# RMS norms scaled by rows and transposed plainly, a weight split in placed pieces, more fillers, and output projections that end in token order

## The chip, the cores and the metric

The kernel is one program on 1 core of a Trainium2 chip. The metric is the device time of one execution in microseconds (us). The engines that matter are TensorE (PE, matmuls, with its weight loads listed as PEld), VectorE (DVE), ScalarE (ACT), GpSimd (POOL) and the DMA queues, which SyncE (SP) issues nearly all. Each engine works through its own queue; engines wait for each other by semaphores.

## The reference, cut to what matters

256 tokens of width 1024 pass two blocks. The first block has two layers, and each layer a mixer (stick-breaking attention in layer 0, retention in layer 1) and a mixture of 16 experts. The second block has an S5 branch and a sparse attention branch, merged, and then a large expert lookup (PEER). Norms stand between all of them.

```python
def first_block(x, c, ...):
    for i in range(2):
        shift, scale, gate = adaln_params(c, ada_w[i, 0], ada_b[i, 0])
        h = x * (1.0 + scale) + shift
        y = stick_breaking_attention(h, w_in, w_out) if i == 0 else retention(h, ...)   # both end in  o @ w_out
        x = layer_norm(ALPHA * x + (1.0 + gate) * y, ln_g[i, 0], ln_b[i, 0])
        shift, scale, gate = adaln_params(c, ada_w[i, 1], ada_b[i, 1])
        y = grouped_moe(x * (1.0 + scale) + shift, ...)      # top 2 of 16 experts in one of 4 groups
        x = layer_norm(ALPHA * x + (1.0 + gate) * y, ln_g[i, 1], ln_b[i, 1])

def rmsnorm(x, g):
    return x * rsqrt(mean(x * x) + 1e-6) * g

def second_block(x, ...):
    proj = rmsnorm(x, norm1_g) @ w_in                        # first rms norm
    ...                                                      # S5 and attention branches, merged
    h = x + merged @ w_out
    h = h + peer_ffn(rmsnorm(h, norm2_g), ...)               # second rms norm, then PEER
    return rmsnorm(h, norm_f_g)
```

## The kernel before, in words

**Tiling.** The 256 tokens are two token tiles, t = 0 and 1, of 128 rows. Between stages the activations lie with tokens on partitions (`x_mid`); for a projection they are transposed in 8 blocks of 128 columns to a tile with the width on partitions. The dense projections split each f32 operand into a high half (an ACT cast to fp32r) and a low half (the difference, by DVE or POOL) and add three matmuls (`split` L148, `mm3` L166). Weights come in pieces of 1 MB; each takes a buffer `w` and two buffers `hl`, of which block 1 has 6 and 6 and the mixers' part of block 2 has 3 and 4.

**Order.** The kernel is traced in program order, and a planner orders each engine's queue by program priority and its own estimate of when work is ready. `issue_after(ins)` (also through `behind()`, L340, for the last DVE instruction traced) keeps what it encloses behind an instruction on that instruction's engine. A tile pool of four PSUM banks, `ps`, serves all short uses, another of four, `y`, the accumulators.

**Output projections** (`proj_out` L427) take the weight two blocks of rows at a time: 4 chunks for stick-breaking attention and for the merge, 8 for retention. In a chunk token tile 0's 12 matmuls come first, then token tile 1's 12, into four accumulators `y[t][half]`. So in the last chunk tile 0 is complete 12 matmuls before tile 1.

**Layer norms** (`layer_norm` L304) follow for each token tile: product with the gate row on DVE (L314), sum with the residual (L316), mean and sum of squares on ACT (L320, L324), the power -1/2 on POOL (L330), the scaling on DVE (L335, or L332 and L333 in the last one, which also applies the gain and bias). `warm` (L172) puts fillers on PE: products with a matrix of ones into a bank that nobody reads; `WA` says how many at each place. A filler is two matmul instructions of 128 columns. After the norms ahead of the experts come 16 transposes, the router's logits, the routing on DVE, and the gather. `moe` keeps 15 MB of expert weights in flight and loads the next piece where a buffer comes free; its first loads take the buffers that `proj_out` gives back.

**RMS norms** (`normed` L993) sum the squares of each token tile on ACT (L1000), take the power on POOL (L1005), and make a diagonal matrix of the row scales (L1007). A matmul of a block of `x` with this diagonal transposes and scales it at once, block by block, both token tiles into one PSUM bank; ACT then writes the high half with the gain (L1012) and DVE the low half (L1013). The first rms norm is called from `mixers` (L1312), which prefetches the first weight `wa[0]` ahead of it, its low half in four DVE pieces (L160), and `wa[1]` behind it. The second is called from `block2` ahead of `peer_scores` (L1414), whose first weight has its low half made by POOL in four pieces (L160).

## Time and profile before

| what | value |
|---|---|
| median of 3 runs | 2079.44 us (2075.39 to 2080.48) |
| profiled execution, own time | 2080.8 us |
| its span, first to last instruction | 2079.0 us |
| mean granted clock of PE | 0.977 |
| PE busy, share of the span | 1970.1 us, 95% |
| PE weight loads | 1531.0 us, 74% |
| DVE | 1218.3 us, 59% |
| ACT | 801.3 us, 39% |
| POOL | 417.7 us, 20% |
| DMA | 496.09 MB, mean 239 GB/s |

The busy times overlap. PE's includes the modelled end of each pipelined matmul, so 95% does not say that PE is at its peak. The chain of waits is the work followed back from the last instruction, at each step to what released it. A granted clock of 1.00 is PE at 2.4 GHz, 0.50 is 1.2 GHz. In a timeline a row merges neighbouring instructions of one kind: its start, its length, the engine, the line, what it writes and reads, and how many.

### The profile page before, as it was taken

How to read it: one execution, taken by the hardware profiler on the slowest of the kernel's cores; microseconds unless marked ns; L12 is line 12 of the kernel's file. 1: busy time of each engine (PE TensorE's matmuls, PEld its weight loads, DVE VectorE, ACT ScalarE, POOL GpSimd, SP SyncE). 2: the span in 40 equal slices, each digit the busy share in tenths (PEclk: the TensorE clock that was granted, in tenths of full speed). 3: DMA queues.
4: the chain of work that ended last, by engine and by line, in shares of the span. 5: the costliest groups of instructions: out<-in, count | busy, mean ns of one | idle time of the engine just before them, and what ended most of it. 6: DMA issues, size and time to landing. Idle time of an engine off the chain costs nothing.

```text
span 2079.0 us, 31873 instructions
## 1 busy us (share of the span) xinstructions
PE 1970.1 (95%) x12566; PEld 1531.0 (74%) x12567; DVE 1218.3 (59%) x2489; ACT 801.3 (39%) x1254; POOL 417.7 (20%) x319
## 2 busy tenths in 40 slices
PE   6999999989999999997888999999999999999998
PEld 4977443339998844335766889999999998888886
DVE  3645321128885422115587569767999986555555
ACT  3444111124454211113333544555444444444444
POOL 1000000002332000000231144544665550000000
PEclk8999999999999899998998999999999999999999
DMA  9797799997875699996332361544554445555554
GB/s 388 270 407 269 293 395 392 395 384 252 312 266 178 241 370 394 396 391 257 132 132 72 131 238 35 161 151 143 171 193 145 153 153 191 186 190 192 189 189 149
DMA packets 155888, 496.09 MB, mean 239 GB/s; under 512 B 10177, under 2 KB 10593, under 8 KB 147153
## 3 DMA queue, kind: packets, MB, share of 16 engines
q1 hardware_dynamic: 152880, 483.42, 64.6%
q0 software_dynamic: 2848, 10.53, 1.4%
q8 instruction: 102, 1.67, 0.3%
q14 instruction: 58, 0.47, 0.1%
HBM read 486.30 MB, written 7.61 MB: 238 GB/s over the span
## 4 chain that ended last, share of the span: by engine, by line
PE 76%; DVE 8%; ACT 2%; issue 2%; DMA 1%; POOL 1%; POOLq 0%; SPq 0%; DVEq 0%; ACTq 0%
PE ps L163 45%; PE y L163 28%; PE y L1200 1%; PE ps L187 1%; DMA w<-moe_w_down 1%; DVE pair L1547 1%; DVE hl L153 1%; DVE et L1471 1%; DVE i L1448 0%; ACT hl L151 0%; POOL hl L160 0%; DVE ps L1193 0%; DVE pos L1459 0%; DVE v L1447 0%; DVE t L725 0%
## 5 line engine op out<-in xcount | busy, mean ns | idle before, releaser
L163 PE MATMUL ps<-hn,pair 128*128 128x256 f32 x3072 | 383.3, 285 | 4.2 <-DVE pair L1547 4.1
L163 PEld LDWEIGHTS ps<-hn,pair 128*128 128x128 f32 x3072 | 373.8, 192 | 5.4 <-DVE pair L1547 4.9
L163 PE MATMUL ps<-w,t 128*64 128x512 f32 x624 | 278.9, 598 | 7.7 <-ACT t L196 2.7
L163 PE MATMUL ps<-hl,t 128*64 128x512 f32 x624 | 279.7, 599 | 4.5 <-DVE t L194 3.1
L1547 POOL TENSOR_TENSOR pair<-raw,pair 128x640 fp32r<-128x640 f32 x128 | 235.9, 1851 | 157.0 <-ACT pair L1545 150.8
L151 ACT CAST hl<-w 128x2048 fp32r<-128x2048 f32 x79 | 150.4, 1903 | 137.0 <-PE ps L163 81.3
L153 DVE TENSOR_TENSOR pair<-raw,pair 128x1024 fp32r<-128x1024 f32 x128 | 156.8, 1225 | 67.2 <-ACT pair L151 67.2
L163 PE MATMUL y<-pair,tmp 128*128 128x512 f32 x768 | 189.7, 395 | 0.0
L163 PE MATMUL y<-pair,eT 128*128 128x512 f32 x768 | 186.5, 391 | 0.0
L163 PEld LDWEIGHTS y<-pair,tmp 128*128 128x128 f32 x768 | 144.4, 188 | 33.9
L163 PEld LDWEIGHTS ps<-w,t 128*64 128x64 f32 x624 | 82.4, 137 | 117.2 <-issue 106.8
L163 PEld LDWEIGHTS y<-pair,eT 128*128 128x128 f32 x768 | 144.2, 188 | 32.4
L1545 ACT CAST pair<-raw 128x1024 fp32r<-128x1024 f32 x128 | 134.2, 1051 | 65.1 <-PE ps L163 24.6
L153 DVE TENSOR_TENSOR hl<-w,hl 128x2048 fp32r<-128x2048 f32 x51 | 118.2, 2318 | 52.8 <-ACT hl L151 49.2
L151 ACT CAST pair<-raw 128x1024 fp32r<-128x1024 f32 x128 | 133.8, 1045 | 1.1 <-issue 1.1
L163 PEld LDWEIGHTS ps<-hl,t 128*64 128x64 f32 x624 | 81.6, 137 | 68.8 <-issue 62.1
L163 PE MATMUL ps<-hl,a 128*128 128x256 f32 x1008 | 130.3, 287 | 1.8 <-ACT hl L151 1.8
L330 POOL TENSOR_TENSOR ln_st<-ln_st,c_mhalf 128x1 f32<-128x1 f32 x8 | 7.9, 982 | 604.0 <-ACT ln_st L327 604.0
L163 PEld LDWEIGHTS ps<-hl,a 128*128 128x128 f32 x1008 | 124.0, 191 | 6.1 <-ACT hl L151 2.0
L725 DVE TENSOR_TENSOR t<-t,ps 128x512 f32<-128x512 f32 x16 | 11.0, 688 | 171.5 <-PE ps L163 171.5
L163 PEld LDWEIGHTS ps<-a,hl 128*128 128x128 f32 x864 | 106.4, 195 | 3.5 <-issue 1.6
L163 PE MATMUL ps<-a,hl 128*128 128x256 f32 x864 | 108.6, 287 | 0.3 <-DVE a L153 0.3
(427 smaller groups left out, 3012.5 us busy)
## 6 DMA issues: line engine op xcount, KB each, us to landing
raw<-peer_u SPq DMA_DIRECT2D x128, 512.0 KB, 3.5
raw<-peer_v SPq DMA_DIRECT2D x128, 512.0 KB, 3.3
w<-ada_w SPq DMA_DIRECT2D x35, 1024.0 KB, 8.3
w<-moe_w_down SPq DMA_DIRECT2D x28, 1024.0 KB, 14.3
hl<-moe_w_down SPq DMA_DIRECT2D x28, 1024.0 KB, 14.2
w<-moe_w_up SPq DMA_DIRECT2D x26, 1024.0 KB, 14.3
hl<-moe_w_up SPq DMA_DIRECT2D x26, 1024.0 KB, 14.3
w<-moe_w_gate SPq DMA_DIRECT2D x24, 1024.0 KB, 14.4
```

Source lines behind the costliest of these rows:

```text
L151: nc.scalar.copy(hi, src)
L153: nc.vector.tensor_tensor(lo, src, hi.bitcast(F32), op=OP.subtract)
L163: self.last_mm = self.nc.tensor.matmul(out, lhsT=lhsT, rhs=rhs, start=start, stop=stop, skip_group_check=True)
L187: self.nc.tensor.transpose(out, in_, self.ident[:in_.shape[0], :in_.shape[0]])
L330: nc.gpsimd.tensor_tensor(st[:, 3:4], st[:, 2:3], self.mhalf[:, 0:1], op=OP.pow)
L725: nc.vector.tensor_tensor(hid, hid, pu, op=OP.mult)
L1200: self.nc.tensor.matmul(py[32 * q:32 * q + 32, :S], lhsT=self.s5_ct[ct][:, 4 * i + q], rhs=ab[q % 2][:, x, ri], start=j == 0, stop=j == 3, ...
L1471: V.tensor_reduce(et[:, 0:2, h], oh.rearrange("p a k j -> p a j k"), axis=AX.X, op=OP.add)
L1545: nc.scalar.copy(up[:, 0], ur)
L1547: lo = eng.tensor_tensor(up[:, 1, ks], ur[:, ks], up[:, 0, ks].bitcast(F32), op=OP.subtract)
```

## The change

`proj_out` keeps the last two chunks of the weight and runs their matmuls together: all 24 of token tile 0, then all 24 of token tile 1, which are queued behind tile 0's. It applies to the two output projections of the first block and to the merge projection. `normed` scales the rows of a token tile on DVE (one instruction of 128x1024 in place of the diagonal), transposes its 8 blocks with PE's transpose into four PSUM banks taken at the start, tile 0 and then tile 1, and then evacuates block by block; DVE's steps and ACT's are held in program order. The first rms norm's weight `wa[0]` has its low half in four DVE pieces at set places: before the norm, after the rows of tile 0, after block 3 and after block 5; `wa[1]` is queued behind the norm on ACT too. Fillers: 5 for 3 after tile 0's sum of squares in every layer norm, 7 and 5 after the two tiles of the last layer norm, 4 after tile 0's squares in each rms norm.

```diff
--- before.py
+++ after.py
@@ -40,8 +40,10 @@
 TH = 1
 LNP = ((0, 1), (1, 1))
 WN = 128
-WA = {4: 3, 5: 3, 6: 3, 7: 3, (2, 0): 1, (3, 0): 3}
+WA = {4: 3, 5: 3, 6: 3, 7: 3, (2, 0): 1, (3, 0): 5}
 LAG = 2
+RW = (4, 0)
+LW = (7, 5)
 ATR = 4
 SCORE = 4.16
 PACE = 2.81
@@ -331,11 +333,19 @@
             if last:
                 V.scalar_tensor_tensor(x[:, t], xh[:, t], st[:, 1:2], grow, op0=OP.add, op1=OP.mult)
                 self.tail = V.scalar_tensor_tensor(x[:, t], x[:, t], st[:, 3:4], brow, op0=OP.mult, op1=OP.add)
+                self.warm(x[:, t], LW[t])
             else:
                 V.tensor_scalar(xh[:, t], xh[:, t], st[:, 1:2], st[:, 3:4], op0=OP.add, op1=OP.mult)
         if not last:
             self.left = [(t, s, x, grow, brow) for t in range(T) for s in (slice(0, 512), slice(512, D))]
         return xh
+
+    def after(self, *ops):
+
+        stack = ExitStack()
+        for op in ops:
+            stack.enter_context(self.tc.issue_after(op.ins))
+        return stack
 
     def behind(self):
 
@@ -401,6 +411,17 @@
         for src in chunks:
             self.done[src.tensor.name, src.offset] = self.wload(src, eng=eng)
 
+    def slices(self, src):
+
+        w, hi, lo = (a.rearrange("p (k n) -> p k n", k=KB) for a in (self.w(), self.hl(), self.hl()))
+        self.nc.sync.dma_start(w, src)
+        self.nc.scalar.copy(hi, w)
+        self.done[src.tensor.name, src.offset] = hi, lo
+
+        def piece(q):
+            self.nc.vector.tensor_tensor(lo[:, q], w[:, q], hi.bitcast(F32)[:, q], op=OP.subtract)
+        return [lambda q=slice(k, k + 2): piece(q) for k in range(0, KB, 2)]
+
     def proj_t(self, src, x, emit, pool=None, eng=None):
 
         wh, wl = self.wload(src, eng=eng)
@@ -428,19 +449,25 @@
 
         nkb = o[0].shape[1]
         W = src.rearrange("(k p) n -> p k n", p=P)
+        held = {}
         for k2 in range(nkb // 2):
             between.get(k2, lambda: None)()
             w, wh, wl = (a.rearrange("p (k n) -> p k n", k=2) for a in (self.w(), self.hl(), self.hl()))
             self.nc.sync.dma_start(w, W[:, k2 * 2:k2 * 2 + 2])
             self.split(wh, wl, w)
-            for t in range(T):
-                for kk in range(2):
-                    k = k2 * 2 + kk
-                    oh, ol = o[0][:, k, t * P:t * P + P], o[1][:, k, t * P:t * P + P]
-                    for hf in range(2):
-                        cs = slice(hf * 512, hf * 512 + 512)
-                        self.mm3(y[t][hf], (oh, ol), (wh[:, kk, cs], wl[:, kk, cs]),
-                                 first and k == 0, last and k == nkb - 1)
+            for kk in range(2):
+                held[k2 * 2 + kk] = wh[:, kk], wl[:, kk]
+
+            if not (last and k2 == nkb // 2 - 2):
+                for t in range(T):
+                    with self.tc.issue_after(self.last_mm.ins) if t and len(held) > 2 else nullcontext():
+                        for k, (h, l) in held.items():
+                            oh, ol = o[0][:, k, t * P:t * P + P], o[1][:, k, t * P:t * P + P]
+                            for hf in range(2):
+                                cs = slice(hf * 512, hf * 512 + 512)
+                                self.mm3(y[t][hf], (oh, ol), (h[:, cs], l[:, cs]),
+                                         first and k == 0, last and k == nkb - 1)
+                held = {}
             self.background(self.rate)
 
 
@@ -990,28 +1017,39 @@
                                     op0=OP.subtract, op1=OP.mult)
 
 
-    def normed(self, x, gcol, hl=None):
+    def normed(self, x, gcol, hl=None, among=()):
 
         self.pieces = PC[1]
         nc, V = self.nc, self.nc.vector
-        xs, scales = self.act8().rearrange("p (t d) -> p t d", t=T), []
+        xs, among = self.act8().rearrange("p (t d) -> p t d", t=T), dict(among)
+
+        def place(name):
+            if name in among:
+                with self.behind():
+                    among[name]()
+        place("first")
+        pts = [self.psum((P, 2, S)) for _ in range(KB // 2)]
         for t in range(T):
-            rs = self.wk.tile([P, 2], F32, name="rms")
-            nc.scalar.activation(xs[:, t], x[:, t], AF.Square, accum_out=rs[:, 0:1])
-            if SM & 4:
-                nc.scalar.activation(rs[:, 0:1], rs[:, 0:1], AF.Identity, scale=1.0 / D, bias=self.eps[:, 1:2])
-            else:
+            rs, junk = self.wk.tile([P, 2], F32, name="rms"), self.t4()
+            nc.scalar.activation(junk, x[:, t], AF.Square, accum_out=rs[:, 0:1])
+            self.warm(junk, RW[t])
+            with self.behind():
                 V.tensor_scalar(rs[:, 0:1], rs[:, 0:1], 1.0 / D, RMS_EPS, op0=OP.mult, op1=OP.add)
             nc.gpsimd.tensor_tensor(rs[:, 1:2], rs[:, 0:1], self.mhalf[:, 0:1], op=OP.pow)
-            scales.append(self.wk.tile([P, P], F32, name="rms_diag"))
-            V.tensor_scalar(scales[t], self.ident, rs[:, 1:2], None, op0=OP.mult)
+            with self.behind():
+                V.tensor_scalar(xs[:, t], x[:, t], rs[:, 1:2], None, op0=OP.mult)
+            place(f"rows{t}")
+            for k in range(KB):
+                self.transpose(pts[k // 2][:, k % 2, t * P:t * P + P], xs[:, t, k * P:k * P + P])
         hi, lo = hl or [self.act8(F32R).rearrange("p (k s) -> p k s", k=KB) for _ in range(2)]
-
-        def each(k, pt):
-            g = gcol[:, k:k + 1]
-            nc.scalar.activation(hi[:, k], pt, AF.Identity, scale=g)
-            self.tail = V.scalar_tensor_tensor(lo[:, k], pt, g, hi[:, k].bitcast(F32), op0=OP.mult, op1=OP.subtract)
-        self.transposed(x, each, scales)
+        for k in range(KB):
+            pt, g = pts[k // 2][:, k % 2], gcol[:, k:k + 1]
+            with self.after(*([self.last_s] if k else [])):
+                self.last_s = nc.scalar.activation(hi[:, k], pt, AF.Identity, scale=g)
+            with self.behind():
+                self.tail = V.scalar_tensor_tensor(lo[:, k], pt, g, hi[:, k].bitcast(F32),
+                                                   op0=OP.mult, op1=OP.subtract)
+            place(f"block{k}")
         return hi, lo
 
 
@@ -1313,16 +1351,14 @@
 
         nc, V, G = self.nc, self.nc.vector, self.nc.gpsimd
         wa, wg = self.io["w_in_a"], self.io["w_in_g"]
-        with self.tc.issue_after(self.tail.ins):
-            self.prefetch([wa[0]], PS)
-        xn = self.normed(x, self.n1g)
+        xn = self.normed(x, self.n1g, among=zip(("first", "rows0", "block3", "block5"), self.slices(wa[0])))
         keep = lambda name, shape: self.wk.tile(list(shape), F32, name=name, bufs=1)
         uT, qT = (self.t4().rearrange("p (i s) -> p i s", i=4) for _ in range(2))
         kiM = self.t4().rearrange("p (i s) -> p i s", i=4)
         kM, qiT = keep("kM", (P, 2, S)), keep("qiT", (P, 2, S))
         v, wi = keep("v2", (P, T, 128)), keep("wi", (P, T, 8))
         ums = self.ums = [self.t4().rearrange("p (q s) -> p q s", q=4) for _ in range(2)]
-        with self.tc.issue_after(self.tail.ins):
+        with self.after(self.tail, self.last_s):
             self.prefetch([wa[1]], PS)
             for a in (kM, kiM, *ums):
                 V.memset(a, 0.0)
```

## Rows read from the trace of the kernel before

**Rows 1.** The page's chain that ended last: shares of the span by engine.
```profile
PE 76%; DVE 8%; ACT 2%; issue 2%; DMA 1%; POOL 1%; POOLq 0%; SPq 0%; DVEq 0%; ACTq 0%
```

**Rows 2.** Windows: span, busy us by engine, granted clock, DMA share, GB/s.
```profile
216.00:220.00 4.00, 4.00 (x29) 4.00 (x30) 2.48 (x8) 1.83 (x6) 0.00 (x0) 0.84 0.00 0
...
228.00:232.00 4.00, 4.00 (x22) 1.39 (x20) 0.00 (x0) 0.45 (x1) 0.00 (x0) 1.00 1.01 372
```

**Rows 3.** Timeline after stick-breaking's projection: start us, us, engine, line, work, count.
```profile
174.27 21.15 PE L163 MATMUL y<-hl,a 128*128 128x512 f32 x92
...
194.77 1.37 DVE L314 TENSOR_TENSOR a<-y,t 128x512 f32<-128x512 f32 x2
...
198.73 0.19 ACT L324 ACTIVATION_READ_ACCUMULATOR t<-a,ln_st 128x1 f32 x1
...
198.83 1.03 ACT L151 CAST a<-a 128x1024 fp32r<-128x1024 f32 x1
...
199.76 0.29 ACT L327 ACTIVATE ln_st<-ln_st,c_eps 128x1 f32<-128x1 f32 x1
...
200.04 1.22 DVE L153 TENSOR_TENSOR a<-a 128x1024 fp32r<-128x1024 f32 x1
...
200.13 1.54 POOL L330 TENSOR_TENSOR ln_st<-ln_st,c_mhalf 128x1 f32<-128x1 f32 x1 [2.29 <-ACT ln_st L327]
...
201.71 0.81 DVE L335 TENSOR_SCALAR a<-a,ln_st 128x1024 f32<-128x1024 f32 x1 [0.45 <-POOL ln_st L330]
...
202.57 1.09 PE L187 MATMUL ps<-c_pack,a 128*128 128x128 f32 x8
```

**Rows 4.** Windows in the two attention seams, columns as in rows 2.
```profile
200.00:204.00 4.00, 3.49 (x27) 2.98 (x27) 2.80 (x5) 1.87 (x4) 1.54 (x1) 1.00 1.04 386
...
704.00:708.00 4.00, 4.00 (x20) 3.67 (x19) 1.82 (x2) 1.68 (x3) 0.00 (x0) 0.50 1.04 406
```

**Rows 5.** Timeline: transposes before retention, and retention's output projection.
```profile
466.75 3.08 PE L187 MATMUL ps<-c_pack,a 128*128 128x128 f32 x12
...
666.08 30.19 PE L163 MATMUL y<-hl,a 128*128 128x512 f32 x132
```

**Rows 6.** Chain that ended last, in order: first expert matmuls of both layers.
```profile
220.42 14.28 PE ps L163 x68
...
724.56 14.28 PE ps L163 x68
```

**Rows 7.** Timeline, last layer norm to the first rms norm.
```profile
963.20 1.65 PE L163 MATMUL ps<-t,c_ones 128*128 128x128 f32 x6 [0.71 <-ACT t L324]
...
965.03 2.48 DVE L333 SCALAR_TENSOR_TENSOR x_mid<-x_mid,ln_st,t 128x1024 f32<-128x1024 f32 x2
...
967.43 2.49 DVE L160 TENSOR_TENSOR hl<-w,hl 128x512 fp32r<-128x512 f32 x4
...
970.13 1.06 POOL L1005 TENSOR_TENSOR rms<-rms,c_mhalf 128x1 f32<-128x1 f32 x2 [4.57 <-DVE rms L1004]
...
971.14 5.78 PE L163 MATMUL ps<-rms_diag,x_mid 128*128 128x128 f32 x32 [6.29 <-DVE rms_diag L1007]
...
973.65 1.75 ACT L1012 ACTIVATE a<-ps,c_pack 128x256 fp32r<-128x256 f32 x4 [4.84 <-PE ps L163]
...
976.13 1.82 DVE L1013 SCALAR_TENSOR_TENSOR a<-ps,c_pack,a 128x256 fp32r<-128x256 f32 x4 [0.20 <-ACT a L1012]
...
976.68 11.77 PE L163 MATMUL ps<-a,hl 128*128 128x256 f32 x96
```

**Rows 8.** Timeline, merge projection to the second rms norm.
```profile
1205.44 10.27 PE L163 MATMUL y<-hl,a 128*128 128x512 f32 x44 [0.69 <-DVE hl L153]
...
1218.35 2.05 PE L163 MATMUL ps<-rms_diag,x_mid 128*128 128x128 f32 x16 [2.64 <-DVE rms_diag L1007]
...
1219.48 5.00 POOL L160 TENSOR_TENSOR hl<-w,hl 128x512 fp32r<-128x512 f32 x4 [1.00 <-ACT hl L151]
...
1222.70 5.99 PE L163 MATMUL ps<-hn,hl 128*128 128x256 f32 x48
```

## The prediction

> **What bounds the kernel now.** I read the page's chain of waits first: of the work that ended last, TensorE (PE) holds 76%, VectorE (DVE) 8%, ScalarE (ACT) 2% [rows 1]. So the edits, which touch no bulk matmul, can win only where that chain leaves PE: the seams between an output projection or an expert stage and the projection after it. Next I read the windows of busy time around the first expert stage, for the DMA share. Between 216 and 220 us nothing moves, since every weight buffer is full; at 228 to 232 the queues carry 372 GB/s at a share of 1.01 [rows 2]. So an expert stage runs at the pace of its weight stream, and that stream goes on only once PE has used the first weights: what is cut from the seam before it moves the whole stage. Then the timelines of the seams, one by one: after the stick-breaking projection [rows 3], the same seam after retention, with windows of both for the clock [rows 4 to 6], the last layer norm with the first rms norm [rows 7], the merge projection with the second [rows 8].
>
> **Output projections in token order, before the first and third layer norms.** The last two weight chunks are held and run as 24 matmuls for token tile 0, then 24 for tile 1. 92 of these matmuls take 21.15 us, 0.230 each [rows 3]. Tile 0 was complete 12 matmuls before the end and is now complete 24 before it: 2.76 us earlier. Tile 1 ends where it did (195.42), and its norm, which the seam waits for, starts at 194.77 as before. What is gained is what tile 0's work cost tile 1 on the shared engines. Two such places stand in the rows. ACT's sum for tile 1 is over at 198.92, but the split of tile 0 (198.83, 1.03 us) stands in front, and the next step starts at 199.76: 0.84 us. Then POOL's power takes 1.54 us while DVE subtracts tile 0's low half (200.04 to 201.26); elsewhere two powers take 1.06, so 0.53 each [rows 3, 7]: 1.01 us. Together 1.85 us. Against it: tile 0's scaling (0.81 us) now ends at about 195.25, across tile 1's start at 194.77: 0.5 us. Net 1.3 us. Bounds: 1.85 above; below, if tile 0's scaling, its copy out of PSUM (about the 0.69 of half of a 1.37 us pair) and its subtraction (1.22) all get in front of tile 1, 2.7 minus 1.85, a loss of 0.9. I take 1.3, as the program lists the norm's own steps ahead of the copy and the split. Retention's seam has the same steps: 2.6 us for both. The last chunk's split costs nothing there: it is on SBUF before tile 0 comes to it. The chunk before the last frees its buffers 12 matmuls later, so two expert weights are loaded 2.8 us later; the idle DMA of [rows 2] covers that, and without that cover the stage would lose 2.8.
>
> **Fillers after tile 0's sum of squares, 3 to 5 in each layer norm.** Two pairs more are four instructions of 0.128 us (16 take 2.05 [rows 8]), 0.5 us, queued on PE behind tile 1's matmuls and ahead of tile 1's transposes, which come 5.8 us after them: free. What they may change is the clock. After retention the granted clock was 0.50 in the seam, the lower level (1.2 GHz), from 704 to 708; at the like place after the stick-breaking projection, 200 to 204, it was 1.00 [rows 4]. From the projection's end to the first long run of expert matmuls it is 724.56 - 696.27 = 28.3 us there and 220.42 - 195.42 = 25.0 here [rows 3, 5, 6]: 3.3 us. With tile 0's part now packed behind the projection, PE stands less, so I expect the fall to come later or not at all, and take half, 1.6 us; the ends are 3.3, and -3.3 if the first seam falls instead.
>
> **The first rms norm.** Before: DVE's last layer-norm step ends at 967.51; then four pieces of the first weight's split (2.49) stand ahead of the rms steps; the power comes at 970.13, the diagonal, 32 matmul instructions from 971.14, the first block out at 973.65, the last low block at 977.95, and the projection, queued behind those 32 on PE, starts at 976.68 [rows 7]. After: one piece (0.62) to 968.1; the small scale about 0.2 (ACT's like-sized reading takes 0.19 [rows 3]), power 0.53, the row scaling 0.81 (as the layer norm's [rows 3]) to 969.7; a second piece to 970.3; the same three steps for tile 1 to 971.95. Its first two transposes (8 take 1.09 us [rows 3], 0.14 each) let ACT start at about 972.4, DVE at 972.85. Then DVE sets the pace: eight blocks of 0.455 (four take 1.82) and two pieces of 0.62 end at 977.75. PE works along with them, three matmuls of 0.123 a block (96 take 11.77), so the first half projection ends at 978.1 instead of 976.68 + 24 x 0.123 = 979.6: **1.5 us**. The second weight's split moves behind it, 2.5 us of DVE and due one weight (5.9 us) of PE work after the first: free. The fillers (10, 24 and 8 instructions, 42 in all) run from 963.2; at half clock, 0.275 each (6 take 1.65), the first ten end at 965.95 and 32 start at 966.3; if the full level is back soon after, they take 32 x 0.128 = 4.1 us, and with tile 0's transposes PE is free at 971.5, before tile 1's rows. If it is not, they end at 975.1, 16 transposes at 0.257 each (12 take 3.08 [rows 5]) follow, and the half projection ends at about 982.3: a loss of 2.7. The upper end is 2.0, with the pieces hidden.
>
> At this step a rule bears on the diagonals that go. The trace shows twelve transposes before retention at 0.257 us each where eight others took 0.136 [rows 3, 5]: both levels of the clock occur around transposes, and no row tells whether they can hold it. The Trainium skill (TensorE: Matmul & The Clock Gate, Part 4: PE-mode transpose) says that the full clock does not engage for TensorE's transposes. By that rule the new transposes are no substitute for the diagonal matmuls; rival 3 below prices this.
>
> **The second rms norm.** Three things cancel. Four of the third chunk's matmuls could run ahead of its low half (44 of 96 were left at 1205.44 [rows 8]); now only tile 0's two may: 0.46 later. The row scaling takes 0.81 where the diagonal with its handoffs took at most 0.48 (from the first power's end, 970.66, to 971.14 [rows 7]), 0.3 or more late, which transposes of one instruction where the diagonals took two return. PE no longer has its projection behind all 32 diagonals (from 1222.70), worth 0.9. But POOL's pieces of that weight end at 1219.48 + 5.00 = 1224.48 and follow the later squares, so the half projection still ends near 1225.7. I take 0, ends -0.5 and +0.9.
>
> **Sum.** 2.6 + 1.6 + 1.5 + 0 = 5.7 us. The profiled execution took 2080.8 us (span 2079.0): 2075.1. That run lies 1.4 above the median of the runs shown, 2079.44, so by the median **2073.7 us**. A difference of 0.3% (6.2 us) is about what a measurement of this kernel can tell from no change.
>
> **Rivals.**
> 1. *The full clock holds through every seam.* All of the 3.3 instead of 1.6, and the slow stretch before retention, where twelve transposes take 3.08 us instead of 12 x 0.136 = 1.6 [rows 3, 5], gives 1.5 too: 8.9 us, 2070.5. For it: one seam of the two already holds through its router. Against it: PE still waits for tile 1's chain.
> 2. *Tile 0's work crowds tile 1 on DVE.* The two token-order seams give nothing, and the clock stays as it is: only 1.5 remains, 2077.9. For it: DVE's queue is in order and tile 0's steps now come when tile 1's start. Against it: the program lists tile 1's norm steps ahead of tile 0's copy and split.
> 3. *No clock from the transposes.* The lower level lasts through the first rms norm: evacuation and transposes (2 x 0.257 a block, 0.51) then keep one pace, but the first half projection's 24 matmuls at twice 0.123 take 5.9 us from about 973.5 and end at 979.4, no gain there. Without clock gains elsewhere 2.6 + 0.2 remain: 2076.6. The Trainium skill's rule above would have it so.
> 4. *Slower: fillers queue ahead of work at half clock.* The place is PE's queue in the seams: 42 instructions stand before the first norm's transposes (-2.7), the stick-breaking seam falls to the lower level as retention's did (-3.3), and the second norm, whose PE now stands between tile 0's and tile 1's transposes, starts its 24 matmuls at half clock (24 x 0.123 = -3.0). Against +2.6 that is -6.4: 2085.8. It decides when the level is still the lower one as the 24 last-norm filler instructions begin. For it: the clock stood low from the layer norm's sums to the diagonals, fillers of 0.275 us included [rows 7]. Against it: the longer filler run starts earlier.
>
> **How the numbers follow.** The forecast 0.42, its own range 2070.5 to 2077: half of it lies over 0.3% below. Rival 1 0.20, rival 2 0.12, rival 3 0.10, rival 4 0.16 (0.10 beyond 0.3%, the rest between). Faster 0.22 + 0.20 = 0.42; the same 0.20 + 0.12 + 0.10 + 0.06 = 0.48; slower 0.10. The range 2069 to 2083 leaves out the best part of rival 1 (0.07) and most of rival 4 (0.12).
>
> **What would show it.** Right: in the timeline after each output projection, tile 0's product on DVE 5.5 us before tile 1's, POOL's power for tile 1 near 0.55 us; the time from the projection's end to the expert matmuls under 25 us at both seams; in the first rms norm the first block out at about 972.4 and the projection's matmuls starting with it. Wrong: transposes that start after 973 behind fillers, an ACT split of tile 0 still ahead of tile 1's sums, a lower clock in the windows of the first seam, or a gain that stands in the seams and is gone at the end of the expert stages.

## The result and the profile after

The changed kernel takes 2099.11 us (median of 6 runs, 2095.10 to 2101.53), the kernel before in the same comparison 2077.57 (6 runs, 2071.14 to 2080.48): a ratio of 1.0102, 95% interval 1.0087 to 1.0117. It is 1.0% slower; forecast were 2073.7, between 2069 and 2083. The profiled execution took 2098.84 us, span 2097.1, mean granted clock 0.974 (before 0.977).

To place the 18 us between the two spans, like instructions of ACT, DVE, POOL and SP were paired between the traces. The shift is how much later such an instruction starts than in the kernel before, as a median for a stretch. A seam is the time between one long run of matmuls and the next. The shift is -1.1 us before the first change acts (versions with equal code there lie between -3.0 and +0.2), grows by 5.7 in the seam after stick-breaking, falls by 1.0 up to the last layer norm, grows by 5.0 in the first rms norm, 7.7 in the second and 1.4 in the expert lookup: 17.8 at the end. So three places have to be explained. In all fences below, timelines have the columns of [rows 3].

**The seam after stick-breaking**, the changed kernel's timeline ([rows 3] are its counterpart):

```profile
185.98 0.29 PE L165 MATMUL ps<-c_pack,ada_sh 128*128 128x16 f32 x2
...
186.66 1.18 PE L165 MATMUL ps<-c_pack,ada_sh 128*128 128x16 f32 x10
...
195.03 1.37 DVE L316 TENSOR_TENSOR a<-y,t 128x512 f32<-128x512 f32 x2 [2.80 <-PE y L165]
...
196.45 0.81 DVE L338 TENSOR_SCALAR a<-a,ln_st 128x1024 f32<-128x1024 f32 x1
197.18 1.22 DVE L318 SCALAR_TENSOR_TENSOR a<-x_mid,a 128x1024 f32<-128x1024 f32 x1
...
200.44 0.29 ACT L329 ACTIVATE ln_st<-ln_st,c_eps 128x1 f32<-128x1 f32 x1
...
200.82 0.55 POOL L332 TENSOR_TENSOR ln_st<-ln_st,c_mhalf 128x1 f32<-128x1 f32 x1 [6.03 <-ACT ln_st L329]
...
201.40 0.81 DVE L338 TENSOR_SCALAR a<-a,ln_st 128x1024 f32<-128x1024 f32 x1 [1.26 <-POOL ln_st L332]
...
202.27 1.97 PE L189 MATMUL ps<-c_pack,a 128*128 128x128 f32 x8 [0.59 <-DVE a L338]
...
205.21 3.59 PE L165 MATMUL y<-r_W,t 128*128 128x16 f32 x16 [0.97 <-DVE t L196]
```

Its windows, columns as in [rows 2]:

```profile
200.00:204.00 4.00, 3.41 (x21) 2.64 (x20) 1.62 (x3) 1.75 (x4) 0.55 (x1) 0.78 1.05 390
204.00:208.00 4.00, 3.03 (x15) 2.79 (x14) 1.15 (x2) 1.87 (x2) 0.00 (x0) 0.50 1.02 407
704.00:708.00 4.00, 3.59 (x29) 2.99 (x28) 2.73 (x3) 2.12 (x6) 1.39 (x1) 1.00 1.05 387
```

Twelve of the router's small matmuls now run inside the projection (185.98, 186.66), so tile 1's product starts at 195.03, 0.3 us later than in [rows 3], although the stretch ahead of the seam ran 1.1 us early. Tile 0's scaling (196.45) stands ahead of tile 1's residual sum. And the clock, 1.00 from 200 to 204 before [rows 4], is 0.78 and then 0.50: tile 1's eight transposes take 1.97 us, not 1.09 [rows 3]. POOL's power for tile 1 is 0.55 us, as the forecast had it. After retention it is the other way round: the clock is 1.00 from 704 to 708, where it was 0.50 before [rows 4].

**The first rms norm** ([rows 7]):

```profile
968.52 2.47 DVE L335 SCALAR_TENSOR_TENSOR x_mid<-x_mid,ln_st,t 128x1024 f32<-128x1024 f32 x2
...
969.95 4.67 PE L165 MATMUL ps<-x_mid,c_ones 128*128 128x128 f32 x24 [0.84 <-DVE x_mid L335]
...
975.35 1.91 PE L189 MATMUL ps<-c_pack,a 128*128 128x128 f32 x16
976.64 0.47 ACT L1048 ACTIVATE a<-ps,c_pack 128x256 fp32r<-128x256 f32 x1 [4.46 <-PE ps L189]
977.15 0.48 DVE L1050 SCALAR_TENSOR_TENSOR a<-ps,c_pack,a 128x256 fp32r<-128x256 f32 x1 [1.93 <-ACT a L1048]
977.66 0.84 ACT L1048 ACTIVATE a<-ps,c_pack 128x256 fp32r<-128x256 f32 x2 [0.55 <-DVE a L1050]
978.17 0.88 DVE L1050 SCALAR_TENSOR_TENSOR a<-ps,c_pack,a 128x256 fp32r<-128x256 f32 x2 [0.54 <-ACT a L1048]
...
978.71 6.24 PE L165 MATMUL ps<-a,hl 128*128 128x256 f32 x48 [1.45 <-DVE a L1050]
...
983.49 3.69 ACT L153 CAST hl<-w 128x2048 fp32r<-128x2048 f32 x2
983.63 0.48 DVE L1050 SCALAR_TENSOR_TENSOR a<-ps,c_pack,a 128x256 fp32r<-128x256 f32 x1 [0.54 <-ACT a L1048]
984.17 0.48 DVE L1364 MEMSET kM<- 128x512 f32 x1
...
987.79 2.43 DVE L162 TENSOR_TENSOR hl<-w,hl 128x512 fp32r<-128x512 f32 x4
...
988.57 2.90 PE L165 MATMUL ps<-a,hl 128*128 128x256 f32 x12 [3.62 <-DVE hl L162]
...
992.61 5.34 PE L165 MATMUL ps<-a,hl 128*128 128x256 f32 x36
```

ACT (L1048) and DVE (L1050) wait for each other from block to block ("0.55 <-DVE", "0.54 <-ACT"): the eight blocks with two pieces take 7.48 us from 976.64 to 984.11; before it was 4.30. Then the second weight is late. Its cast is queued behind the norm, and its low pieces stand behind four memsets; PE stands 3.62 us and goes on at the lower clock (12 matmuls in 2.90 us, 0.24 each). So the loss is at the second weight: the first 24 matmuls end 11.08 us behind the layer norm, before it was 12.30.

**The second rms norm** ([rows 8]):

```profile
1218.85 1.37 DVE L1447 TENSOR_TENSOR x_mid<-y,x_mid 128x512 f32<-128x512 f32 x2 [2.20 <-PE y L165]
...
1224.29 1.38 DVE L1447 TENSOR_TENSOR x_mid<-y,x_mid 128x512 f32<-128x512 f32 x2 [4.07 <-PE y L165]
...
1225.59 0.14 DVE L1037 TENSOR_SCALAR rms<-rms 128x1 f32<-128x1 f32 x1
...
1227.24 0.75 DVE L1040 TENSOR_SCALAR a<-x_mid,rms 128x1024 f32<-128x1024 f32 x1 [1.51 <-POOL rms L1038]
...
1228.72 5.40 POOL L162 TENSOR_TENSOR hl<-w,hl 128x512 fp32r<-128x512 f32 x4
1228.72 1.80 DVE L1040 TENSOR_SCALAR a<-x_mid,rms 128x1024 f32<-128x1024 f32 x1 [0.67 <-POOL rms L1038]
1230.58 1.97 PE L189 MATMUL ps<-c_pack,a 128*128 128x128 f32 x8 [1.44 <-DVE a L1040]
...
1233.06 1.90 ACT L153 CAST hl<-w 128x2048 fp32r<-128x2048 f32 x1
...
1234.99 2.29 DVE L155 TENSOR_TENSOR hl<-w,hl 128x2048 fp32r<-128x2048 f32 x1 [1.28 <-ACT hl L153]
```

Tile 0's sum is there at 1220.2, its squares at 1221.4, yet its small step L1037 comes at 1225.59: `behind()` keeps it behind the last DVE instruction traced, tile 1's sum. Its lead of 4 us is lost. Then tile 1's row scaling takes 1.80 us beside POOL's pieces, where tile 0's took 0.75, and the second query weight's split (1.90 and 2.29) stands between the blocks: from the first block out to the last low block 9.21 us, before 4.13.

### The profile page after: what moved, and what is told of

It is laid out like the page before. It is cut to its first block, busy times and chain, and to the rows that moved or that the text cites. A ratio compares the mean times of both kernels' runs of the same rounds, so it can differ in the third digit from the quotient of the medians.

```text
span 2097.1 us, 31922 instructions
## 1 busy us (share of the span) xinstructions
PE 1979.4 (94%) x12590; PEld 1540.2 (73%) x12591; DVE 1223.1 (58%) x2489; ACT 801.6 (38%) x1254; POOL 412.7 (20%) x319
## 4 chain that ended last, share of the span: by engine, by line
PE 39%; DVE 9%; ACT 2%; issue 2%; POOL 1%; POOLq 0%; DVEq 0%; ACTq 0%
PE y L165 23%; PE ps L165 15%; DVE pair L1583 1%; PE y L1238 1%; DVE i L1484 1%; DVE et L1507 1%; DVE hl L155 1%; DVE v L1483 1%; DVE pos L1495 1%; ACT hl L153 0%; POOL hl L162 0%; DVE big L1591 0%; DVE cand L1490 0%; DVE ps L1231 0%; DVE s L1486 0%
```

## The experiments

Each version was timed against runs of the kernel before on the same chip. Two tables, read from the profiles, hold for all. In the first, growth of the shift against the kernel before, us:

```
                 ratio [95% interval]      start  seam1  to LN  norm1  norm2  lookup  end
changed kernel   1.0102 [1.0087, 1.0117]   -1.1   +5.7   -1.0   +5.0   +7.7   +1.4   +17.8
out_alone        1.0002 [0.9986, 1.0018]   +0.1   +3.9   -3.5   +0.9   +0.5    0.0    +1.1
fill_alone       1.0012 [0.9999, 1.0024]   -2.9   +0.5   -3.9   +0.2    0.0   +2.7    -3.2
norm_alone       1.0051 [1.0033, 1.0068]   -1.8   -0.3   -0.8   +0.3   +7.4   +3.9    +9.2
bank_each        1.0064 [1.0044, 1.0084]   +0.2   +5.2   +0.5   +1.3   +5.2   +2.2   +14.7
wa1_ahead        1.0051 [1.0034, 1.0068]   -3.0   +5.1   -2.4   +0.7   +7.6   +0.7    +8.2
lead_back        1.0065 [1.0048, 1.0081]   -1.6   +5.8   -3.4   +4.6   +2.6   +4.4   +12.3
wq_behind        1.0077 [1.0051, 1.0102]   -1.4   +5.5   -0.5   +5.0   +5.8   +3.0   +17.5
all_set          1.0002 [0.9989, 1.0015]   -1.7   +5.3   -5.4   -3.7   -2.2   +1.2    -6.9
router_held      1.0002 [0.9986, 1.0018]   -1.8   +2.6   -3.5    0.0   +0.5   +2.8    +0.7
merge_only       0.9976 [0.9964, 0.9987]   -3.0   +0.1   -2.3   -4.2   -2.2   +0.8   -11.5
merge_nofill     0.9972 [0.9956, 0.9988]   -1.5   -0.2   -0.7   -2.2   -2.2   +1.2    -6.0
no_fillers       1.0057 [1.0035, 1.0078]   +0.1   +3.6   -7.4   +3.4   +6.9   +0.1    +5.4
norm_fillers     1.0096 [1.0067, 1.0125]   -0.1   +5.4   -9.0   +6.9   +7.7   +1.9   +12.9
seam_fillers     1.0107 [1.0081, 1.0133]   -1.6   +5.1   -3.2   +0.5   +7.7   +2.3   +11.2
```

"Seam1" is the seam after stick-breaking, "to LN" the stretch from there to the last layer norm, with retention's seam. One profile is one execution: "start" and "to LN" differ by up to 5 us between versions whose code is the same there, and the changes between the two norms (up to 1.3) are left out.

"Seam1" is read inside the expert stage behind the seam. At that stage's first matmul, counted from the start of the last output matmul, the kernel before takes 25.66 us, the four other versions without token order there 27.08 to 27.81, and the eleven with it 27.95 to 30.03. The kernel before loses some 1.7 us again further in, where its clock is low from 237.8 to 241.2; so that stretch goes by PE's clock and not only by the weight stream.

The second table: "blocks" from ACT's first block to DVE's last low block, "48" and "96" to the end of the 48th and 96th matmul of the projection, from the end of the last layer norm and of the merge projection's last matmul.

```
                 norm 1: blocks   48     96     norm 2: blocks   48
kernel before            4.30   15.18  20.94            4.13   12.98
changed kernel           7.48   13.95  26.96            9.21   20.05
norm_alone               7.47   15.20  23.76            9.21   20.28
bank_each                4.93   12.39  23.14            3.74   15.16
wa1_ahead                7.47   14.79  22.09            9.21   19.97
lead_back                7.48   13.61  26.45           10.35   15.29
wq_behind                7.48   13.90  26.90            6.27   15.82
all_set                  4.94   12.94  18.70            3.73   11.12
merge_only               4.94   12.58  18.34            3.73   11.12
merge_nofill             4.94   12.97  18.73            3.74   11.12
```

**One part of the change at a time.** `out_alone` is the kernel before with the new `proj_out`:

```diff
+ if not (last and k2 == nkb // 2 - 2):    # hold the last two chunks; tile 0 first, then tile 1
...
```

> The kernel before with the token order of the output projections alone. Theory A (the token order itself costs the first layer norm's seam: tile 0's scaling, split and copies get in front of tile 1's sums, PE then stands and the granted clock falls): the changed kernel's loss of about 5 us between 180 and 225 us appears here, about 2082 in all. Rival (the extra fillers or a chance of the clock did it): the stretch is within 1 us of before, about 2077.

Measured: 2078.96 against 2078.77. The seam loses 3.9 us; 3.5 come back before the last layer norm, in stretches whose clock varies from run to run. So the seam's loss is the token order's; in the total no loss can be told, against the 2082 of theory A.

`fill_alone` has only `WA[(3, 0)]` at 5:

> The kernel before with 5 fillers for 3 after tile 0's sum of squares in the layer norms, nothing else. Theory A: the fillers cost nothing, within 1.5 us of before at the first seam, about 2077. Rival (the fillers stand in front of the transposes and move the fall of the clock): 3 to 5 us slower at the seam after stick-breaking attention, about 2081.

Measured: 2079.49 against 2078.77. From the last output matmul's start to the first expert matmul retention's seam takes 25.60 us, not 28.94, at a clock of 1.00 for its first 20 us; the lookup loses 2.7 again, and no gain is left that can be told.

`norm_alone` has the new norms and neither fillers nor token order:

```diff
-WA = {..., (3, 0): 5}    RW = (4, 0)    LW = (7, 5)    # and proj_out as before
+WA = {..., (3, 0): 3}    RW = (0, 0)    LW = (0, 0)
```

> The kernel before with the new rms norms and the placed weight pieces, without any of the new fillers and without the token order. Theory B (the norms lose by the order of DVE's and ACT's queues and by two blocks in one PSUM bank, whatever the fillers do): about 5 us lost at the first rms norm and 7 at the second, about 2089. Rival (the 24 + 8 fillers ahead of the transposes carry the loss): 1 or 2 us at each, about 2080.

Measured: 2089.97 against 2078.77. The second norm's loss is there whole (7.4); the first's is small (0.3), although its blocks take 7.47 us and the 96 matmuls end 2.8 us later behind the layer norm. The norms alone account for half of the total. In its first norm the first weight runs at the lower clock, so PE stands less long for the second and goes on at the full one:

```profile
971.63 8.12 PE L165 MATMUL ps<-a,hl 128*128 128x256 f32 x48 [0.83 <-DVE a L1044]
...
981.48 1.66 PE L165 MATMUL ps<-a,hl 128*128 128x256 f32 x12 [1.73 <-DVE hl L162]
```

**The norms: what in them costs.** `bank_each` is the changed kernel with a PSUM bank for each block:

```diff
-pts = [self.psum((P, 2, S)) for _ in range(KB // 2)]
+pts = [self.acc.tile([P, 512], F32, name="y")[:, :S] if k % 2 else self.psum((P, S)) for k in range(KB)]
```

> The changed kernel with each transposed block in a PSUM bank of its own (four of them from the accumulators' pool) instead of two blocks in one bank. Theory B1 (ACT waits for DVE's read of the other block in the same bank, so that the two take turns): ACT's and DVE's pass over the eight blocks of the first rms norm falls from 7.5 us to about 5.5 (4.3 before, plus two placed pieces), the changed kernel gets 2 to 5 us faster, about 2095. Rival (the placed pieces and other weights' splits in the queues make the gaps): the pass stays at 7 us or more, about 2099.

Measured: 2092.53 against 2078.77. The timeline of its first norm:

```profile
978.68 0.47 ACT L1048 ACTIVATE a<-ps,c_pack 128x256 fp32r<-128x256 f32 x1 [4.14 <-PE ps L189]
...
979.05 0.47 ACT L1048 ACTIVATE a<-y,c_pack 128x256 fp32r<-128x256 f32 x1
...
979.18 0.48 DVE L1050 SCALAR_TENSOR_TENSOR a<-ps,c_pack,a 128x256 fp32r<-128x256 f32 x1 [1.61 <-ACT a L1048]
979.41 0.48 ACT L1048 ACTIVATE a<-ps,c_pack 128x256 fp32r<-128x256 f32 x1
979.59 0.48 DVE L1050 SCALAR_TENSOR_TENSOR a<-y,c_pack,a 128x256 fp32r<-128x256 f32 x1
```

ACT goes on every 0.36 us without a wait for DVE, and the blocks take 4.93 us, not 7.48: the waits were for the bank, which two blocks shared. The losses fall by 3.7 and 2.5.

`wa1_ahead` puts the memsets behind the second weight's pieces:

```diff
     self.prefetch([wa[1]], PS)
-    for a in (kM, kiM, *ums): V.memset(a, 0.0)
+with self.behind():
+    for a in (kM, kiM, *ums): V.memset(a, 0.0)
```

> The changed kernel with one order turned round behind the first rms norm: the four low pieces of wa[1] come ahead of the four memsets on DVE. Theory C (TensorE stands 3.62 us for these pieces because 3.7 us of memsets are queued ahead of them, and falls to half clock): the stand at about 985 goes or shrinks below 1 us, the 96 matmuls end 3.6 to 5 us earlier, and the whole is 2094 to 2096, about 4 us under the changed kernel. Rival (TensorE would wait for the cast of wa[1] on ACT, which now runs behind the norm, whatever DVE does): less than 1.5 us of the stand goes and the total stays within 2 us of the changed kernel.

Measured: 2090.12 against 2079.33. Its PE:

```profile
975.61 6.24 PE L165 MATMUL ps<-a,hl 128*128 128x256 f32 x48 [1.45 <-DVE a L1050]
983.16 5.99 PE L165 MATMUL ps<-a,hl 128*128 128x256 f32 x48 [1.31 <-DVE hl L162]
```

The stand is 1.31 us instead of 3.62, and the second 48 run at full clock. The norm's loss falls from 5.0 to 0.7: theory C holds, a little short of "below 1 us"; the total lies under the 2094 to 2096 expected.

`lead_back` frees tile 0's small step in the second norm:

```diff
-with self.behind():
+with self.behind() if t or gcol is self.n1g else nullcontext():
     V.tensor_scalar(rs[:, 0:1], ...)
```

> The changed kernel, but in the second rms norm token tile 0's small DVE step (mean and epsilon) is not held behind tile 1's residual add. Theory D (the hold takes tile 0's lead of 4 us away, and the row scaling and transposes of both tiles stand in a row behind the add): rms and power of tile 0 come at about 1222, its rows right behind tile 1's add at 1225.7 in place of 1227.24, tile 1's rows 1.5 us earlier too, and the norm's loss falls from 7.7 to about 6.2; total about 2097.5. Rival (tile 1's own squares, power and rows set the time, since they need the add at 1225.67 anyway): the second norm's loss stays at 7.7 within 0.5.

Measured: 2093.69 against 2079.33. The second norm's loss falls to 2.6, far below the 6.2 expected; the rows come right behind the sum, as theory D had it:

```profile
1220.85 1.38 DVE L1447 TENSOR_TENSOR x_mid<-y,x_mid 128x512 f32<-128x512 f32 x2 [2.70 <-PE y L165]
...
1222.14 0.74 DVE L1040 TENSOR_SCALAR a<-x_mid,rms 128x1024 f32<-128x1024 f32 x1
...
1224.28 0.76 DVE L1040 TENSOR_SCALAR a<-x_mid,rms 128x1024 f32<-128x1024 f32 x1 [0.69 <-POOL rms L1038]
1225.10 1.09 PE L189 MATMUL ps<-c_pack,a 128*128 128x128 f32 x8 [1.06 <-DVE a L1040]
```

More came with it: tile 1's rows take 0.76 us, since POOL's pieces now start behind them, the transposes run at full clock (1.09), and the planner put the second query weight's DVE step behind the seventh block. So the 6.2 counted only the hold and not what followed from it.

`wq_behind` queues that weight's split behind the norm:

```diff
+if h == 1:
+    with self.after(self.tail, self.last_s):
+        self.prefetch([self.io["peer_wq"][1]])
```

> The changed kernel, but the split of the second weight of the expert lookup's queries (ACT cast 1.90 us, DVE difference 2.29 us) is queued behind the second rms norm's last block instead of between its blocks. Theory E (these two stand in the norm's way): the pass over the blocks falls from 9.2 to about 7.5 us, the time that the like pass took in the first norm with its two engines taking turns; the second norm loses about 5.5 to 6 in place of 7.7, if the second weight is not then late by as much. Rival F (the split is only moved: TensorE then stands for the second weight instead): the loss stays within 0.7 of 7.7 and the idle stretch of TensorE shows before the second query projection. Theory E gives a total of about 2097, rival F 2099.

Measured: 2098.73 against 2079.33. The blocks fall to 6.27 us and the norm's loss to 5.8, as theory E has it, but PE then stands 1.6 us for a copy that ACT makes behind the third weight's cast, and the lookup loses 3.0: by the total rival F is right, though the norm's loss did not stay within 0.7 of 7.7 and the wait is not the one it named.

`all_set` takes all four away. It also puts the first query weight's cast ahead of the blocks and its low half on POOL behind tile 1's power, which no version does alone. The part that is new:

```diff
-net.normed(x, net.n2g, hn)
+net.normed(x, net.n2g, hn, among=net.early_w(net.io["peer_wq"][0]))   # load and cast first; low pieces after rows1
-with self.after(*([self.last_s] if k else [])):
+with self.after(*([self.last_s] if k else [self.cast] if gcol is not self.n1g else [])):
...
```

> The changed kernel with every found cause in the two rms norms taken away: one PSUM bank for each block, wa[1]'s low pieces ahead of the memsets, tile 0's small step free in the second norm, the first query weight's cast ahead of the norm's blocks and its low half on GpSimd behind tile 1's power, the second query weight's split behind the norm. If the causes named are the whole loss of the norms, the first norm's drift falls from +5.0 to about -2 to 0 and the second's from +7.7 to between 0 and +2, and the total is about 2083 to 2087, the rest being the seam after stick-breaking (+5 us) and 1.4 us in the expert lookup. The rival, that row scaling and plain transposes are slower in themselves than the diagonals (half clock, 0.75 us of scaling on the path), leaves +3 or more at each norm: 2090 or more.

Measured: 2078.62 against 2079.33. Both norms now gain, 3.7 and 2.2 us, and from the last layer norm's end to the 96th matmul it is 18.70 us, not 20.94. The rival, that row scaling and plain transposes are slower in themselves, falls. The total lies below the 2083 expected and equals the kernel before: what the norms gain, the first seam (+5.3) takes.

**The first seam.** `router_held` is `out_alone` with the router held behind the projection:

```diff
+with net.tc.issue_after(net.last_mm.ins):
     net.router(*net.mod[i, 1][:2])
```

> The kernel before with the token order, and with the router's 16 small matmuls and its DVE steps held behind the output projection's last matmul. Theory H (of the 4.0 us that token order alone lost in the first seam, 1.5 are the 12 router matmuls that the planner put between the projection's): tile 1's product comes 1.5 us earlier in the seam, at the time of the kernel before, and the seam's drift falls from +4.0 to about +2.5; total 2077 to 2079. Rival (the matmuls only change places with other work and the crowding of ACT and DVE sets the time): the drift after the seam stays at 3.5 to 4.

Measured: 2077.42 against 2077.92; the seam loses 2.6, so theory H holds. Its start, 1.77 us early, taken off, this version has tile 1's product at 194.77 and its scaling at 201.56 us, the kernel before at 194.77 and 201.71: the order on DVE and ACT is that of before again. What is left lies behind that scaling, with PE at the lower clock. The same 16 router matmuls show it in `router_held` and, 0.4 us apart, in `merge_nofill` below, whose projection runs chunk by chunk:

```profile
202.14 3.59 PE L163 MATMUL y<-r_W,t 128*128 128x16 f32 x16
```

```profile
202.53 1.96 PE L165 MATMUL y<-r_W,t 128*128 128x16 f32 x16 [0.35 <-DVE t L196]
```

In windows of half a microsecond the first low stretch behind this projection lasts about 3.5 us in the kernel before and in three of the four other versions without token order there, about 10 in nine of eleven with it. It begins 11.2 to 11.7 us behind the last output matmul in those four, 6.0 to 7.5 in the nine. Why is open: apart from the order of the output matmuls, PE's rows of these two profiles are the same in kind and count from 150 to 202 us, 0.3 to 0.6 us apart.

`merge_only` is `all_set` with token order for the merge projection alone:

```diff
-if not (last and k2 == nkb // 2 - 2):
+if not (last and k2 == nkb // 2 - 2 and src is self.io["w_out"]):
```

> The version with the norms' causes taken away, and the token order kept for the merge projection alone; the output projections of stick-breaking and retention run chunk by chunk as before, with 5 fillers. Theory A (token order brings token tile 0's work and its fillers under the projection's end, so TensorE stands longer behind it and falls to half clock about 5 us after it): from the last output matmul to the first expert matmul the first seam takes 26 to 28 us in place of 29.7, the seam after retention about 25.6, as with the fillers alone, and the total is 2072 to 2076, under both kernels. Rival (the first seam's length is a matter of the start and differs from run to run by as much, with or without token order): both seams stay within 1 us of the version before it, 29.7 and 25.0, and the total at 2078 to 2079.

Measured: **2072.20 against 2077.92, ratio 0.9976 [0.9964, 0.9987]**, 12 and 24 runs: faster than both kernels. By the table the first seam loses nothing (27.45 us to the first expert matmul, within the 26 to 28 expected); retention's takes 27.11, not the 25.6 expected. No version has token order for retention alone, or the mended norms without any. The first weights of both norms run without a stand:

```profile
968.75 11.78 PE L165 MATMUL ps<-a,hl 128*128 128x256 f32 x96 [0.32 <-DVE a L1065]
...
1211.19 6.01 PE L165 MATMUL ps<-hn,hl 128*128 128x256 f32 x48 [0.41 <-POOL hl L437]
```

**The fillers.** `no_fillers` is the changed kernel with the fillers of before, `merge_nofill` the same edit in `merge_only`:

```diff
-WA = {..., (3, 0): 5}    RW = (4, 0)    LW = (7, 5)
+WA = {..., (3, 0): 3}    RW = (0, 0)    LW = (0, 0)
```

> The changed kernel with its added fillers left out (3 after tile 0's sum of squares, none in the last layer norm's end and the rms norms). Theory G (the added fillers give the first rms norm a full clock for its transposes and cost nothing): the first norm's 16 transposes take about 4 us in place of 1.9, its first half projection is slower, and the total is the same as the changed kernel's or up to 3 us worse: 2098 to 2102. Rival (fillers queue ahead of work): the first norm's loss falls below 3 us from 5.0 and the total is 2095 to 2097.

> The best version so far (norms' causes taken away, token order for the merge alone) with the added fillers left out: 3 after tile 0's sum of squares, none at the last layer norm's end nor in the rms norms. Theory G (without other obstacles the fillers buy the full clock in the seam after retention, 3 us, and in the first rms norm, where the 96 matmuls of the first two weights take 11.8 us with them): the seam after retention takes about 29 us again, the first norm's transposes run at half clock (about 4 us for 16) and its gain falls from 4.2 to about 1; the total is 2076 to 2079, 4 to 6 us over the version with fillers. Rival (the fillers give nothing, and the gain is the norms' alone): 2071 to 2074.

Measured: 2087.50 against 2077.92 and 2074.58 against 2078.23. In the changed kernel the fillers cost about 0.45% (1.0102 against 1.0057), against theory G, and the total lies under both ranges; in the mended version (`merge_only`) nothing can be told, and the rival stands. The 16 transposes took 3.96 us without them, as G had it, but in the mended version the 96 matmuls end only 0.4 us later without (18.73 against 18.34). Which fillers cost was asked of two more versions, the changed kernel with `WA[(3, 0)]` at 3 (`norm_fillers`) and with `RW` and `LW` at 0 (`seam_fillers`):

> The changed kernel with 3 fillers again after tile 0's sum of squares in the layer norms; the fillers at the end of the last layer norm and in the rms norms stay. Theory K (with token order the two added pairs cost, in the seams: the clock falls earlier behind the stick-breaking projection): the first seam takes about 28 us from the last output matmul to the first expert matmul, as in the two versions with token order and 3 fillers, and the total is 2089 to 2092. Rival (the fillers of the norms cost it): the first seam takes 29.7 and the total stays at 2097 to 2100.

> The changed kernel without fillers at the end of the last layer norm and in the rms norms; 5 stay after tile 0's sum of squares in the layer norms. Theory K: the first seam takes 29.6 to 30.0 us, as in all six versions with token order and 5 fillers, and the total is 2095 to 2098, a little under the changed kernel through the first norm (about 1.6 us). Rival (the fillers of the norms cost it): the first seam takes 29.7 too, but the total is 2088 to 2091.

Measured: 2095.34 and 2098.71 against 2075.72. Either set alone brings most of the loss, and the first seam is 29.64 us with 3 fillers too, so theory K is wrong, and its rival as well. The first norm loses 3.4 and 0.5 without the norms' fillers and 5.0 and 6.9 with them; the rest lies where profiles of equal code differ by as much. The rows show one way in which a faster first weight is paid for. Where its 48 matmuls run at the full clock (the changed kernel, `no_fillers`, `norm_fillers`), PE stands 3.6 us for the second weight, goes on at the lower clock and ends the 96 matmuls 25.3 to 27.1 us behind the layer norm. Where they run at the lower clock (`norm_alone`, `seam_fillers`), it stands 1.7, goes on at the full clock and ends at 23.8. How the loss is divided stays open.

## Why the prediction was wrong, by its steps

**Token order, +2.6.** Wrong in sign at the first seam: a loss of 3.9 alone, where the worst bound was a loss of 0.9. The step that failed is "Tile 1 ends where it did": the planner drew 12 router matmuls into the projection (1.47 us), and without them `router_held` loses 2.6. The gain that was counted came in part: in the changed kernel POOL's power takes 0.55 us, ACT's small step follows the sums at once, and tile 1's steps from product to scaling take 6.37 us, before 6.94, so 0.57 of the 1.3. (In `router_held` it is 6.79: there ACT's split of tile 0 stands in front again and the power takes 1.40.) The 2.6 lie behind the scaling, where PE runs at the lower clock; the text had this only as the far end of the fillers' step ("-3.3 if the first seam falls instead") and as part of rival 4.

**Fillers, +1.6.** Alone they shorten retention's seam by 3.3 us in one profile, the upper end, but the size is not shown: `merge_only`, with 5 fillers too, takes 27.11 us there against 28.94 and 28.95 in the three versions with 3 and no token order, and the total of `fill_alone` is no faster. The failed sentence is "With tile 0's part now packed behind the projection, PE stands less, so I expect the fall to come later or not at all". In the first seam the clock falls 6 to 10.6 us behind the projection with token order and 11.2 us or more without it. In retention's seam the sentence holds: the fall comes 7.0 to 19.2 us behind with token order, 5.7 to 6.0 in those three, and the seam takes 23.48 to 29.28 us. Why the two seams differ is open. The 3.3 itself rested on one profile: `norm_alone` and `merge_nofill`, with the same code up to there, take 1.4 to 1.5 us longer than the kernel before in the first seam and as long in retention's.

**First rms norm, +1.5; measured -5.0.** Two steps failed, and both come due at the second weight, for which PE stands. "Then DVE sets the pace: eight blocks of 0.455 and two pieces of 0.62" is 4.9 us, which `bank_each` shows (4.93); in the changed kernel two blocks share a bank and ACT and DVE take turns in it, 7.48. The Trainium skill (PSUM — Partial Sum Buffer, "PSUM bank collisions raise a hardware error") says that the compiler's scheduler puts a dependency between any two instructions on different engines that touch the same bank in the same 32 partitions, reads too, ACT against DVE among them. The traces agree (7.48 shared, 4.93 apart), and the prediction should have weighed this rule. The other step is "The second weight's split moves behind it: free": PE's time for the first weight was thought to cover it, but it queues behind four memsets and PE stands 3.62 us. The first 24 matmuls, for which the 1.5 was worked out, do end 1.2 us earlier behind the layer norm. With both steps mended (`all_set`) they end 2.2 us earlier (10.06 against 12.30), and so do the 96; the upper end had been 2.0.

**Second rms norm, 0; measured -7.7.** The failed step is "Three things cancel": it counted the scaling and PE's queue, but not that `behind()` holds tile 0 behind tile 1's sum, nor the turns in the bank, nor that the next weight's split falls between the blocks, nor that DVE's scaling doubles beside POOL's pieces. `bank_each`, `lead_back` and `wq_behind` each take 2 to 5 us of it away (1.6 of `wq_behind`'s 1.9 come back in the lookup), and `all_set` turns it into a gain of 2.2.

**Rivals.** Rival 1 falls: the first seam's clock went down. Rival 4 had the sign, and its first-seam part (-3.3) is near the 2.6 found there. Its fillers ahead of the first norm's transposes held those up little: tile 0's waited, but all 16 started at 975.35, 0.1 after tile 1's rows, and the first block is out 5.64 us behind the layer norm, 5.01 in `norm_alone`. Rival 2 shows in part: in the changed kernel tile 0's scaling gets in front of tile 1's sum, 0.7 us. Rival 3 is refuted at its place: 16 transposes right behind 32 fillers took 1.91 us, 0.12 each, the full level, against 3.96 without fillers. In `norm_alone` and `seam_fillers`, without the norms' fillers, the lower level did last and the first 48 matmuls took 8.12 and 8.16 us, not 6.24; in `no_fillers` it did not. The Trainium skill's rule (TensorE: Matmul & The Clock Gate, Part 4: PE-mode transpose) that the full clock does not engage for transposes is not what these rows show; whether transposes can hold it by themselves no run shows.

## What to carry to other kernels

When a matmul that transposes and scales is replaced by scaling and plain transposes, give each block that two engines evacuate a bank of its own, or the engines take turns. An instruction that is "held behind the last one traced" is held behind whatever that is: read each such hold against the moment its inputs are ready, and each prefetch moved behind a norm against all that stands in front of it on the same queue. Four small placements, each worth 2 to 5 us in its norm, hid a gain of 4 us by PE's ends (2.2 and 1.9) or 6 by the shift; so test an idea with its placement mended before giving it up.

## What the runs showed of the hardware

- DVE's scaling of 128x1024 took 1.80 us while POOL's subtraction ran and 0.75 or 0.76 otherwise.
- The first stretch at the lower clock behind one projection lasted about 3.5 us in `merge_nofill` and about 10 in `router_held`, with the same PE rows ahead of it, the order of the output matmuls apart, within 0.6 us.
- Versions with equal code up to there spent 25.01 to 29.28 us in retention's seam (the changed kernel and the six others with token order and 5 fillers): one profile does not price a seam to better than 4 us.
- 16 transposes of 128x128 took 1.91 us behind 32 fillers and 3.96 us without them: they ran at either level of the clock.
